# The order of the blocks of experts: the two blocks of 64 places go fourth and sixth

## The chip, the core and the metric

The kernel runs on one core of one Trainium2 chip. The metric is the time of one execution on the device, in microseconds (us). TensorE does the matrix products (PE in the profile, its weight loads PEld), VectorE (DVE) and ScalarE (ACT) the work on elements, SyncE (SP) issues the loads, and GpSimd (POOL) does little here.

## The reference

One layer of a decoder trunk on 256 tokens of width 2048, in float32. The part that the change touches is the mixture of experts: 32 experts, each a gated MLP of width 256, of which every token takes two.

```
h = layer_norm(ALPHA * x + mix)                       # 256 tokens x 2048
combine = top-1 group, then the two best experts in it, with their weights
g = einsum('td,edf->tef', h, w_gu)                    # 32 experts, 2048 -> 512
act = silu(g[..., :256]) * g[..., 256:] * combine[..., None]
f = einsum('tef,efd->td', act, w_down)                # 256 -> 2048, summed over experts
h2 = layer_norm(ALPHA * h + f)
out = h2 + sigmoid(h2 @ ple_gate_w) * (p @ ple_w)     # the tail
```

In front of it stand the joint input projection, attention beside a convolution, and the output projection.

## The kernel before

A token goes to 2 of 32 experts, so an expert gets few tokens. The kernel sorts the experts by their number of tokens on the chip (`order`) and works in **blocks** of 128 places, the partitions of one product. `BLOCKS` (line 45) lists them as (first rank, places per expert). A block of 32 places takes 4 experts side by side, a block of 64 places takes 2; the ranks 0 to 3, which have most tokens, lie in the two blocks of 64. Block 0, (28, 32), holds four fixed experts whose weights are loaded ahead of time. Blocks 1 to 8 are the run-time ones; their experts' numbers are read from `order` by SP, and the loads go to `gu[e]` and `dn[e]` by that number. Tokens that find no place are treated by a branch ahead of block 7 (`SPILL_BEFORE`), which is passed over when no expert overflows.

One block goes through these steps, named here by the tiles that the profile shows:
- gather (`gather_steps`, lines 795 to 841): VectorE makes a 0/1 matrix `S`, PE multiplies the hidden state with it (`xpb`, line 819, 32 products, which the trace records as 64), and ACT and VectorE write the gathered tokens `XTb`
- upward products (`up`, line 870): per expert 4 loads `gub` of 1 MB (1,048,576 bytes), each used by 4 products `pgb`, which the trace records as 8
- folding, the gate function and the turning of tables (lines 883 to 926: `pgsb`, `natb`, `atb`, `aTb`, `sctb`)
- downward products `dpb` (line 939): per expert 2 loads `dnb` of 1 MB, in two halves of the output's width
- scattering back (lines 945 to 956): `Yhb`, `Ylb`, the products `sob`, and the sum into `acc` on VectorE.

The steps of a block alternate with the gather of the block that follows: after an upward load (64 places) or every second one (32 places), one step of it is taken (line 1164). Block 6 has none to take, as block 7's gather comes behind the branch.

All weight tiles of the experts, `gub` and `dnb` alike, go through one ring of 17 buffers of 1 MB, in rotation (`places`, line 523):

```
while True:
    yield from [ring2] * RING2 + [ringp] * RING
    yield from ring3 * RING3
```

RING2 is 6, RING is 9, RING3 is 2. A load is issued by SP in the order of the program, and waits until the products on the tile that lay in its buffer are done. So the loads run ahead of PE by 17 tiles at most, whatever block they are for. The pool `ring3` is given up as block 7 begins.

The tail, behind block 8, is the last norm, the product with `wgate` (lines 230 to 241) and the output.

Of the kernel before, what the change touches and what calls it, by code (L numbers as in the profile page):

```python
# [41 lines left out]

STATIC = 4

BLOCKS = ((28, 32), (4, 32), (0, 64), (8, 32), (2, 64), (12, 32), (16, 32), (20, 32), (24, 32))

CAPS = [64] * 4 + [32] * 28
SPILL = [(r, n) for r, c in enumerate(CAPS) for n in range(c, min(2 * 128, 2 * 256 // (r + 1) if r < NE - STATIC else 256), 128)]
# [80 lines left out]
def tile_trunk(ctx, tc, xT, x, smalls, consts, win_m, win_v, wout, lnrows,  # L129
# [522 lines left out]
    def first_affine():  # L652
        for c, i in product(range(NCH), range(2)):
            cs = slice(c * CH, (c + 1) * CH)
            r = i * NCH + c
            row = pst([P, CH], f"ln{i}{c}", "g")
            PE.matmul(row, C("ident")[:2 * NCH, r:r + 1].to_broadcast([2 * NCH, P]), rows, start=True, stop=True)
            for t in range(NT):
                if i:
                    DVE.scalar_tensor_tensor(acc(t, cs), row, ALPHA, acc(t, cs), op0=ALU.mult, op1=ALU.add)  # L660
                else:
                    p, h = "hl"[c // 2], 2 * (c % 2) + t
                    accs[t, c] = mpa.tile([P, CH], F32, tag=f"{p}{h}", name=f"acc{t}{c}")
                    DVE.scalar_tensor_tensor(acc(t, cs), z[t][:, cs], ALPHA, row, op0=ALU.mult, op1=ALU.mult)
            yield
# [358 lines left out]
    with in_order():  # L1024
        mvr = norm_stats(st1, bp, "n1")
        warm(W1, "r1")
        sel = selection()
        gs0 = gather_steps(BLOCKS[0], name(0), by=(pm, comb))
        b0 = block(BLOCKS[0], name(0), static=True)
        aff = first_affine()  # L1030
# [33 lines left out]
        next(b0)  # L1064
        gs1 = gather_steps(BLOCKS[1], name(1))
        next(gs1)
# [13 lines left out]
        for _ in range(6):  # L1080
            next(gs1)
        b1 = block(BLOCKS[1], name(1))
        for _ in range(4):
# [5 lines left out]
    def spilled():  # L1089

        over = sp.tile([P, len(SPILL), NT], F32, tag="over", name="over")
        for i, (r, n) in enumerate(SPILL):
            DVE.tensor_scalar(over[:, i], poss[:, :, r], float(n), None, op0=ALU.is_gt)
        many = sp.tile([P, 1 + len(SPILL)], F32, tag="many", name="many")
        DVE.tensor_reduce(many[:, 1:], over, axis=AX.X, op=ALU.add)
        DVE.tensor_reduce(many[:, 0:1], many[:, 1:], axis=AX.X, op=ALU.add)
        total = pst([P, CH], "total", "x")
        PE.matmul(total[0:1, :1 + len(SPILL)], C("ones")[:, 0:1], many, start=True, stop=True)
        flags = rp.tile([1, 1 + len(SPILL)], I32, name="flags")
        DVE.tensor_copy(flags, total[0:1, :1 + len(SPILL)])  # L1100
        return flags
# [38 lines left out]
    flags = spilled()  # L1140
    last = len(BLOCKS) - 1
    for i, shape in enumerate(BLOCKS):
        if not i:
# [226 lines left out]
```

## Time and profile before

| | us |
|---|---|
| median of 3 runs | 934.06 (932.47 to 934.54) |
| profiled execution | 939.12 |
| its span, first to last instruction | 936.9 |
| PE busy | 873.9 (93%) |
| VectorE busy | 509.0 (54%) |
| ScalarE busy | 349.5 (37%) |
| mean rate of the DMAs | 312 GB/s |
| mean granted clock of TensorE | 0.967 of 2.4 GHz |

The span is one profiled execution. Busy time says how long an engine had an instruction under way. PE's 93% is no measure of peak speed, since products overlap. The blocks of experts stand between about 380 and 831 us of it; by the first `pgb` row of each, the run-time block 1 begins at 422.8 us, block 2 at 477.7, block 3 at 523.0, block 4 at 568.9, block 5 at 614.1, block 6 at 661.5, block 7's gather at 712.9 and the last block at 773.5. A row "A <- B" in a list of waits reads: A waited for B. A wait for a DMA is one for a transfer that has not landed; a wait of SP for PE is one for a buffer.

### The profile page before, as it was taken

What the parts mean: (1) busy time and instruction counts of PE and PEld (TensorE: products, weight loads), DVE (VectorE), ACT (ScalarE), POOL (GpSimd) and SP (SyncE); (2) the same over time, 40 slices, a digit from 0 to 9 for tenths busy, and PEclk for the clock granted to TensorE, in tenths of its full rate; (3) what the DMA queues carried; (4) which work ended last, traced back from release to release, by engine and by line L of the source; (5) the groups of instructions that cost most, each with busy time, mean ns of one, the idle gap of its engine ahead of it and who ended that gap; (6) DMA issues with size and microseconds to landing.
All of it is one profiled execution on the core that took longest, in us unless ns stands there. A gap on an engine that the chain in (4) does not pass through costs nothing. (4 is left out here: it accounts for less than half of the span.)

```text
span 936.9 us, 14079 instructions
## 1 busy us (share of the span) xinstructions
PE 873.9 (93%) x5279; PEld 581.1 (62%) x5279; DVE 509.0 (54%) x1090; ACT 349.5 (37%) x684; POOL 4.1 (0%) x16
## 2 busy tenths in 40 slices
PE   7999999999999999999999989998886989899997
PEld 7999879999987887443343434343224423257886
DVE  5989898889988635354322322222123130078875
ACT  6544454666567435320221211121111212237543
POOL 0000000000000000000000000000000000000000
PEclk9999999999999999988999999999977999999999
DMA  9979855444457859998998799999999999998400
GB/s 334 419 207 269 306 186 186 175 142 174 141 180 298 338 180 325 410 410 343 422 421 350 287 409 421 423 389 424 421 423 417 419 421 421 418 416 328 162 32 34
DMA packets 46987, 292.36 MB, mean 312 GB/s; under 512 B 5464, under 2 KB 6120, under 8 KB 13632
## 3 DMA queue, kind: packets, MB, share of 16 engines
q1 hardware_dynamic: 45872, 288.76, 78.3%
q0 software_dynamic: 1040, 2.64, 1.9%
q8 instruction: 43, 0.70, 0.3%
q14 instruction: 32, 0.26, 0.1%
HBM read 287.70 MB, written 3.67 MB: 311 GB/s over the span
## 5 line engine op out<-in xcount | busy, mean ns | idle before, releaser
L878 PE MATMUL pgb<-gub,XTb 128*32 128x512 f32 (+1 forms) x896 | 131.9, 611 | 3.5 <-DMA gub<-in_gu_dram 3.5
L364 DVE SCALAR_TENSOR_TENSOR yall<-u,sml,yall 128x256 f32<-128x256 f32 x240 | 108.7, 478 | 0.3
L819 PEld LDWEIGHTS xpb<-Sb,z 128*128 128x128 f32 x576 | 70.6, 195 | 50.4 <-issue 28.2
L819 PE MATMUL xpb<-Sb,z 128*128 128x128 f32 x576 | 81.8, 290 | 8.1 <-DVE Sb L809 7.1
L826 DVE TENSOR_SCALAR XTb<-xpb,gbc 128x128 f32<-128x128 f32 x72 | 29.5, 409 | 110.2 <-ACT XTb L824 104.0
L939 PE MATMUL dpb<-dnb,aTb 128*32 128x512 f32 (+1 forms) x448 | 83.3, 627 | 0.9 <-DVE aTb L918 0.6
L824 ACT ACTIVATE XTb<-xpb,gbc 128x128 f32<-128x128 f32 x72 | 33.0, 458 | 118.0 <-PE xpb L819 117.9
L878 PEld LDWEIGHTS pgb<-gub,XTb 128*32 128x32 f32 (+1 forms) x896 | 32.4, 114 | 66.2 <-issue 51.4
L689 DVE SCALAR_TENSOR_TENSOR atb<-atb,wb,natb 128x256 f32<-128x256 f32 x9 | 4.3, 480 | 109.9 <-ACT atb L688 109.9
L182 ACT CAST Yhb<-dpb 128x512 fp32r<-128x512 f32 x36 | 19.8, 588 | 106.7 <-PE dpb L939 92.7
L954 DVE TENSOR_TENSOR acc<-acc,sob 128x512 f32<-128x512 f32 x68 | 44.6, 683 | 27.6 <-PE sob L952 27.5
L183 DVE TENSOR_TENSOR Ylb<-dpb,Yhb 128x512 fp32r<-128x512 f32 x36 | 23.5, 686 | 63.0 <-ACT Yhb L182 63.0
L886 ACT COPY pgsb<-pgb 128x512 f32<-128x512 f32 x32 | 18.8, 586 | 100.8 <-PE pgb L878 100.8
L951 PE MATMUL sob<-Yhb,sctb 128*128 128x512 f32 x68 | 32.0, 499 | 16.1 <-DVE acc L954 8.0
L939 PEld LDWEIGHTS dpb<-dnb,aTb 128*32 128x32 f32 (+1 forms) x448 | 19.6, 117 | 41.4 <-issue 36.2
L951 PEld LDWEIGHTS sob<-Yhb,sctb 128*128 128x128 f32 x68 | 12.5, 197 | 50.1 <-issue 21.0
L952 PE MATMUL sob<-Ylb,sctb 128*128 128x512 f32 x68 | 28.0, 440 | 0.1
L907 PE MATMUL natb<-pgsb,cst 128*32 128x512 f32 (+1 forms) x64 | 18.7, 616 | 4.9 <-ACT pgsb L886 4.9
L952 PEld LDWEIGHTS sob<-Ylb,sctb 128*128 128x128 f32 x68 | 12.8, 201 | 6.1 <-DVE Ylb L183 5.3
L1131 PE MATMUL pl<-pw,pT 128*128 128x512 f32 x32 | 15.4, 620 | 0.0
L907 PEld LDWEIGHTS natb<-pgsb,cst 128*32 128x32 f32 (+1 forms) x64 | 3.3, 113 | 16.9 <-ACT pgsb L886 13.5
L1132 ACT COPY z<-pl 128x512 f32<-128x512 f32 x8 | 4.7, 586 | 19.5 <-PE pl L1131 19.5
(2552 smaller groups left out, 1974.9 us busy)
## 6 DMA issues: line engine op xcount, KB each, us to landing
gub<-in_gu_dram SPq DMA_DIRECT2D x112, 1024.0 KB, 17.9
dnb<-in_dn_dram SPq DMA_DIRECT2D x54, 1024.0 KB, 14.4
wo<-in_wout_dram SPq DMA_DIRECT2D x16, 1024.0 KB, 4.8
wg<-in_wgate_dram SPq DMA_DIRECT2D x16, 1024.0 KB, 14.7
earlygu<-in_gu_dram SPq DMA_DIRECT2D x10, 1024.0 KB, 10.4
wv<-in_win_v_dram SPq DMA_DIRECT2D x8, 1024.0 KB, 16.6
wk<-in_win_m_dram SPq DMA_DIRECT2D x8, 1024.0 KB, 4.8
wq<-in_win_m_dram SPq DMA_DIRECT2D x8, 1024.0 KB, 5.0
```

The source lines that it names most:

```text
L182: ACT.copy(h, src)
L183: return DVE.tensor_tensor(l, src, h.bitcast(F32), op=ALU.subtract)
L364: yield DVE.scalar_tensor_tensor(y, u[:, k:k + T], cw[:, c, k:k + 1], y, op0=ALU.mult, op1=ALU.add)
L819: PE.matmul(xp[:, k], z[t][:, kt * P:(kt + 1) * P], S[:, t, :P], start=t == 0, stop=t == 1)
L824: ACT.activation(xs[:, 0], xp[:, 0], AF.Identity, bias=gbc[:, 1, kt:kt + 1], scale=gbc[:, 0, kt:kt + 1])
L826: DVE.tensor_scalar(xs[:, 1], xp[:, 1], gbc[:, 0, kt:kt + 1], gbc[:, 1, kt:kt + 1], op0=ALU.mult, op1=ALU.add)
L878: PE.matmul(pgs_[e][j * M:(j + 1) * M], XT[:, k, e * M:(e + 1) * M], gp[k], start=kt < G, stop=kt >= KT - G, tile_position=(0, j * M) if G ...
L907: PE.matmul(nat[e * M:(e + 1) * M], C(st), folds[e], start=True, stop=True, tile_position=(0, e * M))
L939: last = PE.matmul(dps[n][j * M:(j + 1) * M], aT[:, k, e * M:(e + 1) * M], dp[e][2 * k + n % 2], start=k == 0, stop=k == 1, tile_position= ...
L951: PE.matmul(o, table(n)[:, ts_], Yh[n], start=True, stop=False)
L952: PE.matmul(o, table(n)[:, ts_], Yl[n], start=False, stop=True)
L954: DVE.tensor_tensor(zs, zs, o, op=ALU.add)
```

## The change

The entry (8, 32) moves ahead of (0, 64), and (12, 32) ahead of (2, 64). The blocks of ranks 0 and 2 go from third and fifth in the list to fourth and sixth. Nothing else is edited; the order of the instructions follows from the list by the loop at line 1142.

```
-BLOCKS = ((28, 32), (4, 32), (0, 64), (8, 32), (2, 64), (12, 32), (16, 32), (20, 32), (24, 32))
+BLOCKS = ((28, 32), (4, 32), (8, 32), (0, 64), (12, 32), (2, 64), (16, 32), (20, 32), (24, 32))
```

The first place is SP's queue of loads, from the second expert of block 2 on (`gub21g` is load g of block 2, expert 1; `dnb2ek` is the downward load of expert e, half k). Before:

```order
L178 DMA gub212_5140<-in_gu_dram 128x2048
L178 ISA
L178 DMA gub213_5153<-in_gu_dram 128x2048
L178 ISA
L178 DMA dnb200_5187<-in_dn_dram 128x2048
L178 ISA
L178 DMA dnb210_5189<-in_dn_dram 128x2048
L178 ISA
L178 DMA dnb201_5242<-in_dn_dram 128x2048
L178 ISA
L178 DMA dnb211_5244<-in_dn_dram 128x2048
L675 TENSOR_LOAD order_4187
```

The same rows in the changed kernel:

```order
L178 DMA gub212_5125<-in_gu_dram 128x2048
L178 ISA
L178 DMA gub213_5139<-in_gu_dram 128x2048
L675 TENSOR_LOAD order_4187
L178 ISA
L178 DMA gub220_5148<-in_gu_dram 128x2048
L178 ISA
L178 DMA gub221_5161<-in_gu_dram 128x2048
L178 ISA
L178 DMA gub222_5167<-in_gu_dram 128x2048
L178 ISA
L178 DMA gub223_5181<-in_gu_dram 128x2048
```

Where the last upward load of expert 1 was followed by the four downward loads of a block of two experts and then by block 3, two more experts of block 2 come. A block of 32 places has 24 loads in a row, one of 64 has 12; from the first load of block 6 on the rows stand at the same place in both.

The second place is PE at the border of blocks 1 and 2 (`sob13` scatters block 1, `xpb3` gathers for block 3, `pgb20` is the upward product of block 2, expert 0). Before:

```order
L952 MATMUL sob131_5049<-Ylb13_5032,sctb11_4921 128x512
L878 MATMUL pgb20_5059<-gub200_5060,XTb20_4805 64x512 x4
L819 MATMUL xpb30_5075<-Sb3_5066,z0_73 128x128
L819 MATMUL xpb30_5075<-Sb3_5066,z1_74 128x128
L819 MATMUL xpb30_5075<-Sb3_5066,z0_73 128x128
L819 MATMUL xpb30_5075<-Sb3_5066,z1_74 128x128
L819 MATMUL xpb31_5089<-Sb3_5066,z0_73 128x128
L819 MATMUL xpb31_5089<-Sb3_5066,z1_74 128x128
L878 MATMUL pgb20_5059<-gub201_5069,XTb22_4847 64x512 x4
```

The same rows in the changed kernel:

```order
L952 MATMUL sob131_5051<-Ylb13_5034,sctb11_4921 128x512
L819 MATMUL xpb30_5089<-Sb3_5074,z0_73 128x128
L819 MATMUL xpb30_5089<-Sb3_5074,z1_74 128x128
L819 MATMUL xpb30_5089<-Sb3_5074,z0_73 128x128
L878 MATMUL pgb20_5067<-gub200_5068,XTb20_4805 32x512 x4
L819 MATMUL xpb30_5089<-Sb3_5074,z1_74 128x128
L819 MATMUL xpb31_5112<-Sb3_5074,z0_73 128x128
L819 MATMUL xpb31_5112<-Sb3_5074,z1_74 128x128
L819 MATMUL xpb31_5112<-Sb3_5074,z0_73 128x128
```

The products of block 2 go from 64 rows of output to 32, and the gather for block 3 stands denser between them. Block 2 then has 12 loads more than before, block 3 has 12 fewer.

## Rows read from the trace of the kernel before

**Rows 1.** Page, 40 slices of the span: GB/s that the DMAs moved.
```profile
GB/s 334 419 207 269 306 186 186 175 142 174 141 180 298 338 180 325 410 410 343 422 421 350 287 409 421 423 389 424 421 423 417 419 421 421 418 416 328 162 32 34
```

**Rows 2.** Windows, blocks 2 to 6: stretch, length, engines' busy time, clock, DMA, GB/s.
```profile
477.70:523.00 45.30, 42.25 (x190) 18.76 (x189) 12.76 (x27) 7.89 (x17) 0.00 (x0) 1.00 0.85 343
523.00:568.90 45.90, 41.09 (x293) 17.70 (x292) 13.13 (x29) 9.23 (x20) 0.00 (x0) 1.00 0.97 387
568.90:614.10 45.20, 42.15 (x190) 18.72 (x189) 12.90 (x29) 7.89 (x17) 0.00 (x0) 1.00 1.01 421
614.10:661.50 47.40, 42.58 (x295) 17.94 (x294) 11.99 (x23) 9.24 (x20) 0.00 (x0) 0.96 1.00 407
661.50:705.70 44.20, 36.27 (x223) 9.90 (x222) 8.58 (x15) 5.62 (x11) 0.00 (x0) 0.85 1.01 421
```

**Rows 3.** Windows, four stretches from block 2 to block 8.
```profile
500.00:520.00 20.00, 17.76 (x61) 6.67 (x60) 6.44 (x14) 3.84 (x9) 0.00 (x0) 1.00 0.66 258
520.00:540.00 20.00, 18.99 (x148) 9.89 (x150) 6.26 (x13) 4.64 (x10) 0.00 (x0) 1.00 0.91 335
620.00:640.00 20.00, 18.11 (x147) 7.05 (x145) 2.29 (x6) 4.46 (x9) 0.00 (x0) 1.00 0.97 384
640.00:820.00 180.00, 154.17 (x895) 58.76 (x896) 36.87 (x74) 32.80 (x67) 0.00 (x0) 0.91 1.01 420
```

**Rows 4.** Waits of SP, 477 to 540 us: in total, times, longest.
```profile
SPq L178 <- PE pgb L878: 34.8, 16, 4.4
SPq L178 <- PE dpb L939: 16.9, 4, 8.5
```

**Rows 5.** Waits of PE in 420:661, 661:706 and 706:832 us: in total, times, longest.
```profile
PE atpb L916 <- DVE atb L689: 5.0, 5, 1.0
...
PE pgb L878 <- DMA gub<-in_gu_dram: 3.5, 4, 1.4
...
PE xpb L819 <- DVE Sb L809: 7.1, 1, 7.1
...
PE dpb L939 <- DMA dnb<-in_dn_dram: 0.4, 1, 0.4
```

**Rows 6.** Timeline of PE in block 6: start, length, instruction, idle before it.
```profile
661.48 10.51 PE L878 MATMUL pgb<-gub,XTb 128*32 128x512 f32 x96
672.65 1.06 PE L878 MATMUL pgb<-gub,XTb 128*32 128x512 f32 x8 [0.67 <-DMA gub<-in_gu_dram]
...
675.13 1.07 PE L878 MATMUL pgb<-gub,XTb 128*32 128x512 f32 x8 [0.56 <-DMA gub<-in_gu_dram]
677.62 1.64 PE L878 MATMUL pgb<-gub,XTb 128*32 128x512 f32 x8 [1.42 <-DMA gub<-in_gu_dram]
680.11 1.94 PE L878 MATMUL pgb<-gub,XTb 128*32 128x512 f32 x8 [0.85 <-DMA gub<-in_gu_dram]
```

**Rows 7.** Windows of tile pgb on PE: upward products of blocks 3 and 6.
```profile
523.00:546.20 23.20, 15.66 (x128) 1.00 0.93 352
661.40:682.10 20.70, 16.21 (x128) 0.90 1.01 421
```

**Rows 8.** Windows: rest of block 3 and of block 6.
```profile
546.20:568.90 22.70, 18.15 (x102) 6.78 (x102) 9.42 (x20) 4.37 (x10) 0.00 (x0) 1.00 1.01 424
682.10:705.90 23.80, 19.39 (x88) 5.99 (x88) 7.96 (x13) 3.87 (x8) 0.00 (x0) 0.80 1.01 423
```

**Rows 9.** Timeline of PE: gather inside the rest of block 3.
```profile
551.18 1.16 PE L819 MATMUL xpb<-Sb,z 128*128 128x128 f32 x8
552.17 0.28 PE L837 MATMUL wpb<-cst,Swb 128*128 128x1 f32 x2
```

**Rows 10.** Windows of tile xpb: gather inside block 3.
```profile
523.00:568.90 45.90, 9.00 (x64) 7.67 (x64) 3.27 (x8) 3.67 (x8) 1.00 0.97 387
```

**Rows 11.** Tile gub over the whole span: time from issue to landing.
```profile
DMA to landing us min/median/max: 5.0/17.9/20.9
```

**Rows 12.** Chain that ended last, in order of time: block 8.
```profile
798.89 17.44 DMA dnb<-in_dn_dram
```

## The prediction

> **What bounds the kernel now.** I read the page's row of transfer rates first, then windows cut at the block borders, then the waits, then the timeline where a wait stands.
>
> The rates [rows 1] show two regimes. Up to the middle of the span they jump about; from slice 20 (468 us) on they stand near 420 until the gate weights run out, with a dip in slices 21 and 22 and a small one in slice 26. The 28 experts picked at run time are streamed in this part, 6 loads of 1 MB (1.0486 million bytes) each. So it looks bound by transfers. The waits say otherwise: between 661 and 706 us PE waited 3.5 us for expert weights, in 4 places, and after that 0.4 us once [rows 5]; from 420 to 661 us the list of its waits names no DMA, and the longest of it is 5.0 us on VectorE [rows 5]. PE is the bound almost everywhere, and the stream only just keeps up with it. It fails in one place, block 6 (seventh in the order). There PE takes the first 12 loads (96 records, 8 a load) in 10.5 us without a gap, and from then on gets one load each 2.5 us with gaps in between [rows 6].
>
> Why the loads are late there is told by the blocks before it [rows 2]. At the undisturbed 421 GB/s of those rows a load takes 1.0486/0.421 = 2.49 us. A block of 32 places uses 24 loads, a block of 64 places 12, and both take PE some 45 to 46 us: 45.3 and 45.2 for blocks 2 and 4 (64 places), 45.9 and 47.4 for blocks 3 and 5 (32 places). So a block of 64 leaves room for 18.2 loads and uses 12, one of 32 for 18.4 and uses 24. The ring of 17 buffers evens this out, unless it is full when a block of 64 begins. In block 2 it is: the transfers run at 258 in 500–520 us and 335 in 520–540 [rows 3], while SP, which issues the loads, waits for PE to free buffers, 16.9 us of it in 4 waits for the downward products alone [rows 4]. The time in which nothing was moved is 20 x (422-258)/422 = 7.8 us, 20 x (422-335)/422 = 4.1 and, behind block 4, 20 x (422-384)/422 = 1.8: together 13.7 us, or 5.5 loads.
>
> **The ledger of the ring, before.** Stock means loads that have landed and are not used. It is nothing at 672.0 us, where the gaps of block 6 begin. Landed from 477.7 us until then, by rate times length [rows 2]: 14.8 + 16.9 + 18.1 + 18.4 + 4.2 (10.5 us of block 6) = 72.4; used 12 + 24 + 12 + 24 + 12 = 84. So the stock at 477.7 us was 11.6, and it went 14.4, 7.3, 13.4, 7.8 at the borders, then to nothing. A transfer that finds the DMAs free takes 5.0 us [rows 11], two loads' time; so the DMAs run dry when 15 of the 17 buffers hold unused loads. Inside block 2, at 509 us, its 8 upward loads were used: 11.6 + 31.3/2.49 - 8 = 16.2, over 15, as the stall says.
>
> **The change part by part.** It exchanges the second and third and the fourth and fifth of the run-time blocks. Block 2 becomes 32 places, 3 becomes 64, 4 becomes 32, 5 becomes 64; blocks 1, 6, 7 and 8 keep their experts and their place. By instruction nothing is added or taken away: the same 72 loads stand on SP between block 1 and block 6, in another order, on the same 17 buffers, and PE's rows from block 6 on stand where they stood. The gather of the next block, 64 records, goes with the place and costs the same 9.0 us of PE [rows 10] in either kind of block. So PE's own time over blocks 2 to 5 is that of before, 183.8 us, give or take the 1.5 us that block 5 took longer than block 3 at a clock of 0.96 [rows 2].
>
> The ledger with the new order, at 2.49 us a load throughout: block 2 starts with 11.6, lands 18.4, uses 24: 6.0 left. Block 3: + 18.2 - 12 = 12.2. Block 4: + 18.4 - 24 = 6.6. Block 5: + 18.1 - 12 = 12.7, where before there were 7.8. The fullest moments, after the upward loads of the blocks of 64, are 6.0 + 12.6 - 8 = 10.6 and 6.6 + 12.6 - 8 = 11.2, under 15: the 13.7 us of idle transfers go. The emptiest are the ends of the upward part of blocks 2 and 6. Block 2 wants its sixteenth load at 23.2 us [rows 7] and has 11.6 + 9.3 = 20.9: 4.9 to spare, 12 us. Block 6 (which gathers nothing) wants it after 15.7 us of products and has 12.7 + 6.3 = 19.0: 3.0 to spare, 7.5 us. Nothing waits.
>
> What PE gets back in block 6. Its upward part took 20.7 us; the same 128 records in block 3 were busy for 15.7 [rows 7]: 5.0 us. The rest of the block took 23.8 us at a granted clock of 0.80, where block 3 took 22.7 at 1.00 with 1.4 us of gather inside (1.16 and 0.28) [rows 8, 9]: 23.8 - 21.3 = 2.5 us, which I also count, since the low clock began with the gaps (0.90 over the upward part). The other way round, 44.2 - (45.9 - 9.0 - 0.3) = 7.6 against 7.5. With the 0.4 us of block 8 [rows 5]: 7.9 us.
>
> The Trainium skill speaks to that second term: its page "TensorE: Matmul & The Clock Gate", section "HAM oscillation — how this bites in real kernels", says that waits for transfers between groups of products throw the array to half rate and that the next group pays for it. The trace agrees: 1.00 in block 3, 0.80 behind the gaps of block 6, a mix of the levels 2.4 and 1.2 GHz [rows 8]. Without that rule the sum would be 5.4 us, with it 7.9.
>
> What is late next. Behind block 6 PE has 7.1 us without work at the branch around the spill code [rows 5], which stays. Blocks 7 and 8 run with the stream right behind PE (420 on average, never idle [rows 1, 3]); the chain ends block 8 on a load of 17.4 us [rows 12], of which the queue ahead of it is 12.4. The stream comes 13.7 us earlier and PE 7.9, so the stream gains 5.8 us of lead, and the end is PE's. The tail of 105 us is products alone and moves as a whole.
>
> The profiled execution took 939.12 us (span 936.9): 939.1 - 7.9 = 931.2. The median of the runs is 5.1 us under the profiled time, so I forecast 934.06 - 7.9 = 926.2. Bounds of the terms: low 5.4 us (the clock stays down in block 6 for another reason); high 7.9 + 1.5 (no low clock in block 5) = 9.4, and 13.7 if PE could follow the stream to the end, which only a gain of clock in blocks 7 and 8 (0.91 over 640–820 us [rows 3]) would allow.
>
> **Rivals.**
> 1. The stream runs out at block 6 all the same. It decides at 400 GB/s: to have no gap, block 6 must begin with 16 - 6.3 = 9.7 loads, so 9.7 + 72 - 11.6 = 70.1 must land in the 183.8 us of blocks 2 to 5, 2.62 us each. Before, 68.2 landed, at a mean of 389. For it speaks that the margin between 400 and 421 is small; against it, that every stretch with loads queued shows 419 to 424. Time 930 to 934, by how much is missing. The Trainium skill has a rule for this side: "DMA: Bandwidth & Descriptors", section "Where 436 GB/s comes from", says that HBM binds a core at about 358. By that figure, as an estimate, block 6 would begin with next to nothing and the change would be worth nothing; the 421 of the rows decides against it.
> 2. Slower: two blocks of 32 in a row now follow the ring's refill, and block 2 runs dry. Place: its upward products, some 490 to 501 us. Price: if loads land over 12 us later than my ledger has them (4.9 loads), PE meets gaps there as it did in block 6, 7.5 us with the clock, and block 6 keeps its own, since the lateness exceeds its 7.5 us too: 934.1 + 7.5 = 941.6. For it: the stock of 11.6 is reckoned back over 184 us from rounded rates. Against it: an error of 4.9 in 72 would be 7%, and the full ring of block 2 confirms 15 or more at 509 us.
> 3. More than forecast: the clock dips of blocks 5, 7 and 8 go too, as PE has a denser stretch ahead of them: 934.1 - 11 = 923. Nothing in the rows ties these dips to the stream.
>
> **How the numbers follow.** Forecast 0.70 (its own range 924 to 929), rival 1 0.14, rival 2 0.07, rival 3 0.09. A measurement of this kernel tells about 0.2%, 1.9 us, from no change: between 932.2 and 935.9 is "same". Faster: forecast, rival 3 and a third of rival 1, 0.83; same: most of the rest of rival 1, 0.10; slower: 0.07. The range leaves rival 2 and the far half of rivals 1 and 3 out: 922.5 to 932.5.
>
> **What would show it.** Right: 500–540 us at about 420; PE's waits for expert weights gone from block 6; block 6 at 36 to 37 us and a clock near 1.00; blocks 2 to 5 ending near 661 us as before. Wrong: waits on expert weights in block 2 or 6, a low rate under the blocks of 64 in their new places, or block 7 to 8 giving the time back by waits on transfers.

## The result and the profile after

| | before | changed |
|---|---|---|
| median of the runs, us | 933.26 | 921.60 (920.62 to 922.06) |
| profiled execution, span, us | 936.9 | 919.2 |
| mean granted clock of TensorE | 0.967 | 0.989 |

The ratio is 0.9879, with a 95% interval of 0.9858 to 0.9900: 11.7 us faster by the medians, 9.3 to 13.3 by the interval. The forecast was 926.2 with a range from 922.5, so the direction was right and the size was not: the time lies 0.9 us under the range, 4.6 us under the forecast. (The 933.26 has one run more than the 934.06 that the prediction started from.)

The page of the changed kernel has one row that answers to [rows 1], GB/s in 40 slices:

```profile
GB/s 335 419 220 265 308 206 184 149 173 151 171 166 232 395 158 324 347 419 421 420 422 422 420 422 420 423 420 423 421 422 416 419 422 421 415 420 298 172 24 34
```

From slice 18 on nothing dips any more, until the gate weights run out in slice 36. The windows at the block borders (columns as in [rows 2]; then blocks 7 and 8):

```profile
473.00:518.90 45.90, 40.94 (x292) 17.80 (x292) 12.97 (x29) 9.34 (x20) 0.00 (x0) 1.00 1.01 421
518.90:564.10 45.20, 42.15 (x189) 18.73 (x188) 12.67 (x27) 7.89 (x17) 0.00 (x0) 1.00 1.01 422
564.10:610.00 45.90, 41.08 (x293) 17.68 (x292) 13.14 (x29) 9.23 (x20) 0.00 (x0) 1.00 1.01 422
610.00:655.20 45.20, 42.16 (x190) 18.73 (x189) 11.97 (x23) 7.89 (x17) 0.00 (x0) 1.00 1.01 422
655.20:690.40 35.20, 30.59 (x223) 9.78 (x222) 8.75 (x15) 5.62 (x11) 0.00 (x0) 1.00 1.01 422
697.40:755.40 58.00, 53.14 (x357) 27.15 (x358) 15.64 (x39) 13.15 (x29) 0.00 (x0) 0.97 1.01 420
755.40:813.70 58.30, 52.30 (x265) 17.12 (x264) 10.52 (x18) 13.12 (x24) 0.00 (x0) 1.00 1.02 417
```

Blocks 2 to 5, now 32, 64, 32 and 64 places, take 45.9, 45.2, 45.9 and 45.2 us, with 421 to 422 GB/s under each. Block 6 takes 35.2 us at a clock of 1.00, where it took 44.2 at 0.85 [rows 2]. Two windows over the downward parts of the blocks of 64 answer to the holes of [rows 3]:

```profile
545.00:565.00 20.00, 18.63 (x69) 7.12 (x68) 9.24 (x18) 3.22 (x7) 0.00 (x0) 1.00 1.01 423
640.00:660.00 20.00, 18.94 (x98) 7.03 (x99) 8.22 (x13) 3.44 (x7) 0.00 (x0) 1.00 1.01 422
```

SP's own waits, against [rows 4], would not have told this. In the downward part of block 3, from 541 to 565 us, they are (total, times, longest):

```profile
SPq L178 <- PE dpb L939: 11.0, 4, 7.4
SPq L178 <- DMA gub<-in_gu_dram: 6.0, 4, 2.0
```

SP still waits four times for the downward products to free buffers, as it did in block 2 before (16.9 us), and yet 423 GB/s flow: the loads that it has already issued last through the wait. A wait of SP becomes a hole only where the rate falls.

PE's waits in block 6, and from there to the end of block 8, against [rows 5] (total, times, longest):

```profile
PE sob L951 <- ACT Yhb L182: 1.4, 2, 0.7
```

```profile
PE dpb L939 <- DMA dnb<-in_dn_dram: 1.8, 2, 1.3
...
PE pgb L878 <- DMA gub<-in_gu_dram: 0.9, 1, 0.9
```

In block 6 the longest entry is ScalarE, no transfer. The upward part runs through, as the timeline shows (first and last rows of it; against [rows 6]): 14.8 us from 655.2 to 670.0.

```profile
655.20 11.37 PE L878 MATMUL pgb<-gub,XTb 128*32 128x512 f32 x104
...
666.89 3.14 PE L878 MATMUL pgb<-gub,XTb 128*32 128x512 f32 x23
```

But 2.7 us of waits for weights stand in block 8, where there were 0.4: one of the signs that the prediction named for being wrong. PE has caught up with the stream at the very end. That is the trace of what the prediction missed.

The last load of the experts' weights shows where the end hangs. Its issue, its time to landing, and the last downward products from the timeline (start, length), in the kernel before:

```profile
L973 SPq DMA_DIRECT2D dnb<-in_dn_dram x1: 1562/1562/1562, 811.4 to 811.4; - x1
DMA to landing us min/median/max: 15.3/15.3/15.3
824.86 3.77 PE L939 MATMUL dpb<-dnb,aTb 128*32 128x512 f32 x30
```

The same in the changed kernel:

```profile
L973 SPq DMA_DIRECT2D dnb<-in_dn_dram x1: 1559/1559/1559, 794.5 to 794.5; - x1
DMA to landing us min/median/max: 15.3/15.3/15.3
806.44 5.30 PE L939 MATMUL dpb<-dnb,aTb 128*32 128x512 f32 x30
```

Before, the load lands at 826.7 us and the products end at 828.6; in the changed kernel, at 809.8 and 811.7. Both times PE ends 1.9 us behind the last landing. So already in the profile that the prediction was read from, block 8 could not have ended earlier unless the last load came earlier too.

The whole phase, from the start of block 2 to the end of block 8, as one window, in the kernel before:

```profile
477.70:831.20 353.50, 313.70 (x1799) 128.71 (x1799) 87.04 (x178) 65.83 (x138) 0.00 (x0) 0.95 0.99 404
```

The same phase as one window in the changed kernel:

```profile
473.00:813.70 340.70, 302.41 (x1798) 127.05 (x1799) 86.95 (x178) 66.25 (x138) 0.00 (x0) 0.99 1.01 420
```

Length times rate is 353.5 x 404 = 142.8 MB before and 340.7 x 420 = 143.1 MB after. The bytes are the same, the stream just stands still no longer: the phase is 12.8 us shorter. The rest of the 17.7 us between the two spans (4.7 us ahead of block 2, which began at 477.7 and at 473.0, and 0.2 in the tail) lies where the change has no hand. Ahead of block 2 the execution of before had more low clock: from 380 us to the start of block 1 the granted clock was 0.88 before and 0.96 in the changed kernel.

### The profile page after: what moved, and what is told of

It reads as the page before. It is cut to its first block, busy times and chain, and to the rows that moved or that the text cites. A ratio compares the mean times of both kernels' runs of the same rounds, so it can differ in the third digit from the quotient of the medians.

```text
span 919.2 us, 14080 instructions
## 1 busy us (share of the span) xinstructions
PE 857.5 (93%) x5279; PEld 578.2 (63%) x5279; DVE 509.0 (55%) x1090; ACT 349.7 (38%) x684; POOL 4.1 (0%) x16
## 5 line engine op out<-in xcount | busy, mean ns | idle before, releaser
L939 PE MATMUL dpb<-dnb,aTb 128*32 128x512 f32 (+1 forms) x448 | 80.1, 599 | 2.4 <-DMA dnb<-in_dn_dram 1.8
L951 PE MATMUL sob<-Yhb,sctb 128*128 128x512 f32 x68 | 29.8, 468 | 16.1 <-DVE acc L954 8.0
L952 PEld LDWEIGHTS sob<-Ylb,sctb 128*128 128x128 f32 x68 | 11.9, 188 | 5.8 <-DVE Ylb L183 5.3
L878 PE MATMUL pgb<-earlygu,XTb 128*32 128x512 f32 x88 | 11.9, 681 | 0.0
```

The source lines that it names most:

```text
L878: PE.matmul(pgs_[e][j * M:(j + 1) * M], XT[:, k, e * M:(e + 1) * M], gp[k], start=kt < G, stop=kt >= KT - G, tile_position=(0, j * M) if G ...
L939: last = PE.matmul(dps[n][j * M:(j + 1) * M], aT[:, k, e * M:(e + 1) * M], dp[e][2 * k + n % 2], start=k == 0, stop=k == 1, tile_position= ...
L951: PE.matmul(o, table(n)[:, ts_], Yh[n], start=True, stop=False)
L952: PE.matmul(o, table(n)[:, ts_], Yl[n], start=False, stop=True)
```

## The experiments

The question was what sets the end of block 8. **Stream theory**: the last load of the expert weights, so that the gain is the transfer time that was lost before, some 12 us. **PE theory**, that of the prediction: PE, so that the gain is what block 6 loses and the clock behind it. Each kernel was timed in turn with the kernel before, on the same chip.

### Both kernels again

> The kernel before, unchanged, profiled and timed once more, to see what of its low clock comes back. If the low clock in blocks 5, 7 and 8 belongs to the order of the blocks (or to the gaps of block 6), this profile shows 1.0 us or more of it in the same blocks again, and block 6 at 44 us. If it falls by chance, it stands in other places, and blocks 5 and 7 may take 45.9 and 58.0 us here. Time against before: 0 within 1.5 us.

> The changed kernel, unchanged, profiled and timed once more. Both theories: 10 to 13 us under before, the DMAs at 420 GB/s from block 2 to the end, block 6 at 35.2 us. Stream theory (the end of block 8 is set by the last load): PE waits 2 to 3 us for expert weights in block 8 again. PE theory (the 5.8 us of lead that I predicted for the stream): no such wait in a second profile.

Measured: the kernel before against itself 1.0006 (0.9989 to 1.0023), which is the noise. The changed kernel 922.87 against 933.68, ratio 0.9877 (0.9854 to 0.9900). A third time:

> The changed kernel, unchanged, beside the order fourth and seventh on one chip. 10.5 to 12 us under before; its profile ends 109 to 110 us behind the landing of the last weights of the experts, unless the clock dips of this execution make PE later than the stream.

Measured: 920.44 against 932.96, 0.9883 (0.9851 to 0.9914). The gain repeats, 10.8 and 12.5 us by the medians. (10.8 is just inside what both theories gave, 10 to 13; 12.5 lies 0.5 over the 10.5 to 12 of the last expectation.)

The second profile of before has a span of 928.1 us, 8.8 under the first, with a clock of 0.985. All of that lies ahead of block 2, which begins at 468.8 in place of 477.7. Its waits of PE for weights behind block 6 (total, times, longest):

```profile
PE dpb L939 <- DMA dnb<-in_dn_dram: 1.8, 2, 1.3
PE pgb L878 <- DMA gub<-in_gu_dram: 1.7, 2, 1.4
```

The last transfer in its chain of waits (start, length):

```profile
788.55 19.76 DMA dnb<-in_dn_dram
```

So in this execution the kernel before waits 3.5 us in block 8 for weights, with block 6 at 45.3 us as ever. In the profile that the prediction rested on there were 0.4 us: its clock was lower in blocks 5 and 7 (0.96 and 0.92, against 1.00 and 0.96 in the second), so PE came later and had less to wait for. The phase from block 2 to 8, as one window of this second profile, is as long as in the first, though:

```profile
468.80:822.40 353.60, 309.76 (x1798) 126.79 (x1797) 86.64 (x177) 65.81 (x138) 0.00 (x0) 0.97 0.99 405
```

It is 353.6 us at 405 GB/s, and at a clock of 0.97 in place of 0.95: the same length at another clock, so the stream set it. The same window in the two repeats of the changed kernel gives 343.9 and 342.4 us; the first repeat:

```profile
471.80:815.70 343.90, 307.80 (x1798) 129.03 (x1798) 87.06 (x177) 65.86 (x138) 0.00 (x0) 0.96 1.01 419
```

The second repeat:

```profile
471.20:813.60 342.40, 306.37 (x1798) 128.62 (x1799) 86.99 (x177) 65.93 (x138) 0.00 (x0) 0.97 1.01 420
```

In both, the list of PE's waits names no weights, as its clock dipped (0.96 and 0.97 over the phase). In the first repeat PE ends 3.9 us behind the last landing, 2.0 later than the stream would let it; in the second it ends 1.9 us behind it, as in the first profile, and its span ends 109.9 us behind that landing, as expected. Against my expectation for the stream theory, then, the waits of block 8 aren't always there: in the changed kernel the two bounds lie within some 3 us of each other, and the clock of the execution decides which comes last. The dips of blocks 5 and 7 that the first profile of before showed are not in the second one (45.9 and 58.3 us there), and block 7 takes 60.7 us at a clock of 0.92 in the first repeat of the changed kernel: they come and go in either kernel.

### One pair exchanged alone

```
e_first:  (28, 32), (4, 32), (8, 32), (0, 64), (2, 64), (12, 32), (16, 32), (20, 32), (24, 32)
e_second: (28, 32), (4, 32), (0, 64), (8, 32), (12, 32), (2, 64), (16, 32), (20, 32), (24, 32)
```

> Only the first pair exchanged: the blocks of 64 places fourth and fifth, behind each other. By the ledger the stock is 11.6, 6.0, 12.2 as in the changed kernel, but the second block of 64 begins with 12.2 and is full at its downward part (12.2 + 12.6 - 8 = 16.8): some 3 loads of transfer time are lost there, 6 to 8 us, and block 6 begins with about 9.8, which is just what it needs. Stream theory (gain = transfer idle removed): 5 to 7 us under before. PE theory (gain = gaps of block 6 and the low clock that follows): 9 to 12 us under before, as the change.

Measured: 933.49 against 933.68, 0.9997 (0.9976 to 1.0017): no gain at all. Windows of its profile, the phase and three at the second block of 64:

```profile
472.20:826.10 353.90, 308.82 (x1798) 126.19 (x1799) 86.58 (x177) 65.81 (x138) 0.00 (x0) 0.98 0.99 406
580.00:600.00 20.00, 17.76 (x70) 6.87 (x66) 4.71 (x14) 3.47 (x8) 0.00 (x0) 1.00 0.86 349
600.00:620.00 20.00, 18.99 (x112) 9.80 (x110) 8.22 (x15) 3.91 (x8) 0.00 (x0) 1.00 0.77 285
620.00:640.00 20.00, 18.02 (x148) 6.78 (x147) 1.72 (x4) 4.33 (x10) 0.00 (x0) 1.00 0.97 380
```

The hole has only moved: 20 x (73 + 137 + 42)/422 = 11.9 us of transfer time are lost, where it was 13.7 before. My ledger had 6 to 8. It charged a block with its loads evenly; but a block of 32 that follows begins slowly, as the gather stands between its first four loads (in the timeline they are used from 608.9 to 620.3 us), so the ring stays full there too (the second window). As priced ahead of the run, the stream theory's gain is too large by that error; with the hole as measured it gives 1.8 us, which lies inside the interval of what came (1.6 slower to 2.2 faster). The PE theory's 9 to 12 were wrong by more, but they rested on the same ledger: block 6 has all its gaps here (PE's waits for weights from 640 to 705 us):

```profile
PE pgb L878 <- DMA gub<-in_gu_dram: 5.1, 5, 1.4
PE dpb L939 <- DMA dnb<-in_dn_dram: 1.4, 2, 0.9
```

With 6.5 us of gaps left there, the PE theory gives no gain either. So this run shows what two blocks of 64 in a row cost, and decides nothing between the theories.

> Only the second pair exchanged: the blocks of 64 places third and sixth. The idle transfers of block 2 stay (12 us), the 1.8 us behind block 4 go; by the ledger the stock at the start of block 6 is 8.6 against 7.8 before and 9.7 needed. Stream theory: 1 to 2.5 us under before. PE theory: block 6 keeps most of its gaps, 2 to 4 us under before.

Measured: 931.45 against 933.68, 0.9975 (0.9957 to 0.9993), 2.2 us. Windows of its profile, the phase and two at block 2:

```profile
475.90:826.60 350.70, 308.19 (x1798) 126.75 (x1795) 86.74 (x177) 65.98 (x138) 0.00 (x0) 0.97 0.99 406
500.00:520.00 20.00, 17.65 (x62) 7.04 (x62) 8.55 (x19) 3.60 (x8) 0.00 (x0) 1.00 0.64 242
520.00:540.00 20.00, 19.80 (x160) 9.90 (x163) 4.37 (x10) 4.44 (x10) 0.00 (x0) 1.00 0.94 347
```

12.1 us are lost at block 2 (8.5 and 3.6), and the second hole is closed. The stream theory's 1 to 2.5 us is what came; the PE theory's 2 to 4 isn't excluded. Neither half of the change is worth much alone: in this kernel the blocks of 64 must stand apart, and neither right behind the full ring.

### The dose of the stream

```
 dp[e] = weights_of("dn", e, hf)
+if name == "b4" and 4 * hf + e < 3:              # 6 in the second kernel
+    load(srcs[e][1][hf], f"extra{e}{hf}")
```

> The changed kernel with three more loads of 1 MB in block 4, into tiles of the ring that nothing reads: 7.5 us more for the stream (3 x 2.49), nothing more for PE. PE theory (my prediction: the stream has 5.8 us of lead at the end): 0 to 2 us over the changed kernel. Stream theory (the last load sets the end): 5 to 7.5 us over it, PE waiting for weights in block 6 or 8.

Measured: 927.97 against 934.28, 0.9932 (0.9906 to 0.9959), so 6.3 us under before, and 4.5 to 6.2 over the changed kernel by the two repeats. That is at the lower end of the stream theory's 5 to 7.5, or just under it, and far over the PE theory's 0 to 2. Its phase as one window:

```profile
471.50:820.70 349.20, 307.76 (x1798) 127.37 (x1799) 86.97 (x178) 65.81 (x138) 0.00 (x0) 0.97 1.01 420
```

All its waits of PE for weights in that phase:

```profile
PE dpb L939 <- DMA dnb<-in_dn_dram: 3.7, 4, 1.5
PE pgb L878 <- DMA gub<-in_gu_dram: 1.9, 2, 1.4
```

> The changed kernel with six more loads of 1 MB in block 4 that nothing reads: 14.9 us more for the stream, nothing more for PE. Stream theory: 12 to 15 us over the changed kernel, twice what three loads cost. PE theory: with the 5.8 us of lead that I predicted, 7 to 9 us over it.

Measured: 935.29, against 920.44 for the changed kernel beside it: 14.9 us, which is the 14.9 of six loads. Its phase as one window:

```profile
473.40:830.00 356.60, 313.39 (x1799) 128.67 (x1799) 86.96 (x177) 65.90 (x138) 0.00 (x0) 0.95 1.01 420
```

The clock of this execution was low as well (0.95). Both kernels move 420 GB/s over the phase, so the loads added no hole: they cost their own transfer time. A lead of 5.8 us, as I predicted it, would have swallowed most of three loads. There is no such lead. The PE theory falls here, for the changed kernel.

### The stream made shorter

```
+elif name == "b7" and hf == 1:
+    dp[e] = firsts[e]
 else:
-    dp[e] = weights_of("dn", e, hf)
+    dp[e] = firsts[e] = weights_of("dn", e, hf)
```

> The kernel before with four loads fewer in block 7, behind the gaps of block 6: the second half of its downward products uses the weights of the first half again (columns 1024 to 2047 of what block 7 gives are not the reference's). The stream is 10 us shorter from there, while block 6 keeps its gaps and its 44 to 45 us. PE theory (the gain is what block 6 loses): 0 to 1 us under before. Stream theory: the waits of block 8 go, 3 to 6 us under before, PE's work being the bound from there on.

Measured: 928.33 against 934.28, 0.9924 (0.9898 to 0.9951): 6 to 7 us, with block 6 as badly off as ever (PE's waits for weights in that block):

```profile
PE pgb L878 <- DMA gub<-in_gu_dram: 4.3, 4, 1.4
PE dpb L939 <- DMA dnb<-in_dn_dram: 1.9, 2, 1.5
```

Its phase as one window:

```profile
473.30:824.40 351.10, 309.20 (x1798) 126.51 (x1798) 86.78 (x177) 65.66 (x137) 0.00 (x0) 0.96 0.99 404
```

So in the kernel before too the stream sets the end, some 6 us behind where PE could be, though PE has already lost its time in block 6. Behind block 6 this kernel's list of waits names no transfer. (This one profile had a phase of 351.1 us, at a clock of 0.96 and PE-bound; it was the slowest of the seven runs, so the timed runs are the better witness.) That is at the upper end of the 3 to 6 us that the stream theory gave, or just over it. PE's order is not quite that of before, as the products `pl` and `pgb` alternate otherwise in block 8. That is worth under 1 us: block 8 takes 54.2 us here at a clock of 1.00, and 54.4 and 55.0 in the two profiles of the order fourth and seventh below, which have block 8's products in the old order, no wait for weights in it, and the same clock.

> The changed kernel with four loads fewer in block 7 (the second half of its downward products uses the weights of the first half again; columns 1024 to 2047 of what block 7 gives are not the reference's), PE's instructions as before. The stream is 10 us shorter. If the stream alone is the bound of the changed kernel: 10 us under it. If PE is close behind: 1.5 to 4 us under it, PE without any wait for weights in block 8. If PE is the bound: the same.

Measured: 918.00, against 920.44 for the changed kernel beside it: 2.4 us, ratios to before 0.9828 (0.9804 to 0.9852) and 0.9883 (0.9851 to 0.9914). The two intervals just touch, so the 2.4 are hardly clear of the noise. PE has no wait for weights left. Its phase as one window:

```profile
474.90:813.70 338.80, 302.85 (x1797) 126.85 (x1798) 86.84 (x178) 65.87 (x137) 0.00 (x0) 0.98 1.01 418
```

10 us less stream buy some 2.4 at most: in the changed kernel PE is right behind the stream. The landing of the last load and the end of the last downward products, read as above, put the profiles side by side (us):

| | last load landed | last products end | behind it |
|---|---|---|---|
| before | 826.7 | 828.6 | 1.9 |
| before, second profile | 818.7 | 820.6 | 1.9 |
| before, four loads fewer in block 7 | 813.1 | 821.8 | 8.7 |
| changed | 809.8 | 811.7 | 1.9 |
| changed, first repeat | 809.2 | 813.1 | 3.9 |
| changed, second repeat | 809.1 | 811.0 | 1.9 |
| changed, four loads fewer in block 7 | 801.7 | 811.1 | 9.4 |

Only where the stream was made shorter does PE end far behind it.

> The changed kernel with four loads fewer: the second half of the downward products of block 4 uses the weights of the first half again, so the part of the output that block 4 gives to columns 1024 to 2047 is not the reference's. The stream is 10 us shorter, PE's work the same. PE theory: the same time as the changed kernel, within 1 us. Stream theory with PE close behind: 1 to 4 us under it, until PE's own work is the bound, with no wait of PE for weights in block 8. Stream alone: 10 us under it.

Measured: 914.75 against 934.28, 0.9815 (0.9770 to 0.9859), 6 to 8 us under the changed kernel; one of its six runs took 925.8 us, the others 911.7 to 916.4. This run tells less than it was meant to: with its weights already there, the second half of block 4's downward products moved ahead in PE's order, and blocks 4 and 5 took 87.0 us in place of 91.1, as their two windows show:

```profile
562.70:608.90 46.20, 42.65 (x298) 18.23 (x292) 12.96 (x29) 9.24 (x20) 0.00 (x0) 1.00 1.01 422
608.90:649.70 40.80, 38.66 (x186) 17.54 (x186) 12.09 (x24) 7.99 (x17) 0.00 (x0) 1.00 1.01 418
```

So 4 us of it are PE's. The one above, with block 7, moves PE's order far less and replaces it.

### Another order

```
e_36: (28, 32), (4, 32), (8, 32), (0, 64), (12, 32), (16, 32), (2, 64), (20, 32), (24, 32)
```

> The blocks of 64 places fourth and seventh in the list. By the ledger the stock at the block borders is 11.6, 6.0, 12.2, 6.6, 0.9, and block 5 wants its sixteenth load when 15.9 are there: PE waits a little there, the DMAs never run dry. Stream theory: the same time as the changed kernel, within 1.5 us. PE theory: over it by what it waits in block 5 and what the clock loses there, 1 to 4 us.

Measured: 920.50 against 934.28, 0.9854 (0.9825 to 0.9883). Its phase as one window:

```profile
471.30:813.20 341.90, 303.55 (x1798) 126.49 (x1799) 86.64 (x177) 66.14 (x138) 0.00 (x0) 0.99 1.01 420
```

PE's waits for weights in that phase:

```profile
PE pgb L878 <- DMA gub<-in_gu_dram: 1.8, 3, 1.0
...
PE dpb L939 <- DMA dnb<-in_dn_dram: 0.6, 2, 0.4
```

PE waits 2.4 us along the way, the DMAs move 420 GB/s all through, and the phase is 341.9 us. The 1 to 4 us over the changed kernel that the PE theory gave did not come. Since this ratio was better than the changed kernel's, the two were run side by side:

> The blocks of 64 places fourth and seventh, beside the changed kernel on one chip. Stream theory: no difference beyond 1.5 us either way, since the DMAs are never dry in either order. If the order fourth and seventh is better by its own: 1.5 to 3 us under the changed kernel again.

Measured: 920.94 against 920.44 for the changed kernel, 0.9869 (0.9847 to 0.9891) against 0.9883. No difference. It beats the kernel before by as much as the change does, and neither beats the other: both orders that keep the DMAs from running dry end at the same place. (Others were not run.)

## Why the prediction was wrong

- **The ledger: right.** In blocks 2 to 6 the new order neither lets the DMAs run dry nor PE wait for weights; 13.7 us of lost transfer time were forecast to go, and the phase fell by 12.8 in the profiles. (For `e_first` the same ledger was too low by 4 to 6 us, as told above.)
- **Blocks 2 to 5: right.** 182.2 us against the 183.8 that I kept.
- **Block 6: mis-sized.** It gave back 9.0 us, not the 7.5 of the sum. I took block 3 less its gather as the measure, 36.6 us; the block without a gather takes 35.2. The gather costs a block of 32 10.7 us, more than the 9.3 of its own records. PE does not wait more for it (4.8 us idle in block 4 of the changed kernel, 4.6 in block 6); but at the same clock of 1.00 the upward products are busy for 15.7 us in block 4 and 14.8 in block 6, the downward ones for 9.4 and 8.3. Why they take longer beside a gather, no run here shows.
- **The bound at the end: the step that failed.** "The stream comes 13.7 us earlier and PE 7.9, so the stream gains 5.8 us of lead, and the end is PE's." Three loads more cost 4.5 to 6.2 us, six cost 14.9: there is no lead. The term at fault is the 0.4 us by which PE was held up at the end of before. It was taken from one execution in which low clock in blocks 5 and 7 had made PE late, and there it looked like a PE that the stream could not hold. The second profile of before has 3.5 us there, and the kernel before without four loads behind block 6 is 6 to 7 us faster. The end is the later of two, stream and PE, and before it was the stream's. The stream's term (12 to 13 us) was the gain as long as PE could follow, and PE could: between the two profiles its way grew shorter by 9.0 in block 6, 1.6 in blocks 2 to 5, 0.2 at the branch and 2.6 in block 7, less 0.6 in block 8. Of these only block 6 belongs to the change; the clock dips of blocks 5 and 7 are luck of the two executions. In the second profile of before they are missing, and the 3.5 us of waits stand in their place. The window of block 7 in the kernel before, against 58.0 us in the changed one:

```profile
712.90:773.50 60.60, 55.70 (x356) 27.68 (x357) 15.79 (x39) 13.16 (x29) 0.00 (x0) 0.92 1.01 420
```

- **The range.** The 13.7 us stood in the text as an upper bound, "if PE could follow the stream to the end", with only rival 3 (11 us, 0.09) on that side, and the range stopped at 11.6. The sum of the stream and the sum of PE were two estimates of the same end; I gave the smaller one nearly all the weight, on the ground that only a gain of clock in blocks 7 and 8 would let PE follow. That condition was wrong too: in the second repeat of the changed kernel the clock over blocks 7 and 8 is 0.93, as before, and PE still ends with the last load, its phase 11.1 us shorter. The excess of the profiled time over the median (5 us), which the prediction took off, is no sign of it either way: the 8.8 us between the two profiles of before lie ahead of block 2.
- **Rival 1 and rival 2**: neither came. 420 GB/s held, and block 2 had no wait for weights.
- **Rival 3**: its time, 923, is near by luck: the dips of blocks 5 and 7 that it needs are also missing from the second profile of before, and one is there in a profile of the changed kernel.
- **The term for the low clock in block 6: right in kind.** Without gaps block 6 has a clock of 1.00, with them 0.85 [rows 2], and 0.89 in the second profile of before. The Trainium skill, "TensorE: Matmul & The Clock Gate", section "HAM oscillation — how this bites in real kernels", says that waits for transfers between groups of products bring half rate. The trace agrees, though the waits of the page's kernel are longer than ours, which last 1.4 us at most.

## What to carry to other kernels

Where a stream of loads runs beside an engine, reckon both ends apart, the transfer time from bytes, rate and the holes in it, and the engine's from its work; the later one counts, and a hole in a saturated stream is lost for good, whatever the engine waits for at the moment. Work that uses few loads per time belonged here where the ring is empty, that is, behind work that uses many, and two such pieces apart. How long an engine waits in one execution does not tell how much earlier it could have ended: here 0.4 us in one profile were 3.5 in the next. Look at when the last load lands, and take a second profile before calling the end the engine's.

## What was not expected of the hardware

The stream is steadier than PE. Over some 340 us it moved 419 to 420 GB/s in the three profiles of the changed kernel, and 420 in those with more loads. The same PE instructions took 340.7 to 343.9 us there (2.7 of the 340.7 are waits for weights), and short stretches of low clock fell in other blocks each time: block 7 took 58.0 us at 0.97 in one and 60.7 at 0.92 in the next. The span of the kernel before was 936.9 us in one profile and 928.1 in the other, with all of the difference ahead of block 2, where the first had the lower clock (0.88 against 0.95 from 380 us to block 1); in the changed kernel it was 919.2, 921.2 and 919.0.
